# One softmax block for the second query block of the sliding attention, in a two-layer hybrid trunk on one core

## The chip, the cores and the metric

The kernel runs on one core of a Trainium2 chip. The core's engines each work through an instruction stream of their own, in order, and meet through semaphores: TensorE (PE, matrix products and transposes), VectorE (DVE), ScalarE (ACT), GpSimd (POOL) and SyncE (SP, which here issues weight loads). The metric is the device time of one execution in microseconds; lower is better.

## The reference, cut to what matters

A residual stream of 256 tokens with 1024 channels passes through two layers. Each layer projects the normalised stream once (about 12,800 columns), feeds three mixers with it (a Mamba-2 scan "ssd" with 16 heads in 4 groups, a sliding-window attention "swa" with 16 query heads and 4 key heads, a forgetting attention "fox" with 16 heads), projects and merges the three, and adds an output projection. Everything is float32. The change is in the sliding attention:

```python
# blocks of 128 queries; each sees its own and the previous block of 128 keys
scores = einsum(q_block, [previous keys, own keys]) * 64 ** -0.5     # 128 x 256 per head
diff = qi + 128 - sj
mask = (diff >= 0) & (diff < 128) & (key position >= 0)
scores = where(mask, scores, -inf)
probs  = softmax(concat([scores, sink]))[..., :-1]                    # the sink is one logit per head
out    = einsum(probs, [previous values, own values]) * silu(z)
```

The window is 128 wide. Query i of the second block therefore sees the keys j > i of the first block and the keys j <= i of its own: two triangles that together hold exactly one key for each column j. The first query block sees only the lower triangle of its own keys.

## The kernel before, in words

**Weights and dense products.** SP loads raw weights (`load_part`, up to 6 parts ahead), ACT rounds them to a high part (`hi`, L291), DVE subtracts to get a low part (`lo`, L292), and PE forms three products for each dense one (hi*hi, lo*hi, hi*lo) into PSUM tiles of the tag `mm`. Four parts are kept split ahead of use. These dense products are most of PE's work.

**PSUM.** There are eight banks of 128 x 512 float32. Three rotate under the tag `mm` (`pmm`, L75 to 76), five under `mx` (`pmx`, L78 to 79). `mx` serves all that is not a dense product: scores, transposes, value products, the scan, small sums. Each call of `pmx` takes the next of five tiles; the framework makes its first writer wait for the readers of the tile's former content.

**The attention quads.** `attn_quad` (L587 to 684) handles four heads and is called by `swa_quad` (four a layer) and `fox_quad` (four a layer). Its steps:
1. Four banks of `mx` take the scores of four heads, for query block 0 against 128 keys and for block 1 against 256 keys.
2. For each head and block, one fused DVE operation (L615) multiplies by -1/8, adds a mask or bias, takes the minimum with the sink's negative logit (swa only) and writes the result to an SBUF tile `pp`, the row minimum into `nm`. ACT then takes the exponential from `pp` to `pp` with row sums (L621).
3. For swa the sink's exponential joins the sums (L625 to L628); a reciprocal (L630) and a multiplication with 0.5 (L633) normalise `pp`.
4. After a pause `D_SOFT` (7.0), PE transposes `pp`: twelve 128 x 128 blocks in three banks (six, a pause `D_SOFT2`, six more). ACT copies each bank to SBUF (L652).
5. After `D_EVAC`, the value products of two quads are formed together, one in a bank of `mx`, one of `mm`, and DVE multiplies them onto the gate (L676).

**Others that use `mx` around it.** `ssd_group` (L804 to 862, four a layer): transposes of x for t=0 and t=1 (L816), each read by a DVE multiply (L817); the products of B and C, "cb products" (L842), read by three DVE multiplies (L845); the y products (L857), read by L860. `decay_logits` (L714 to 763): three small results in three banks, copied by ACT (L751, L756 and one after it). `group_norm` (from L904): sums of squares, read by L909. `to_hT` (L297): transposes of the stream in halves, read by ACT (L291) and DVE (L292). The start (from L1350) transposes x in quarters (`turn`, read by L1376) and runs filler transposes.

**What sets the order.** PE's order is written out by a planner in the kernel: it keeps a clock of PE costs, launches the steps above as coroutines, and lets each resume when its pause (`D_...`, in us of PE work) has passed, so that dense products stand between the score products and the transposes. Tokens limit how many quads or scan groups are open; a budget (`BUDGET`) limits how much is put between dense blocks. After the start, the order on DVE, ACT and POOL comes from the framework's scheduler. SP's order of loads follows the planner's feed. The masks (`wmask`, L203 to 210) are made on POOL at the start.

Of the kernel before, what the change touches and what calls it, by code (L numbers as in the profile page):

```python
# [28 lines left out]
T_PP, T_SSD, T_BIAS = 1, 1, 1  # L29
N_RAW, N_SPLIT = 6, 6  # L30
AHEAD = 4
WARM = 7
# [15 lines left out]
def hybrid_trunk(  # L48
# [5 lines left out]
    nc = tc.nc  # L54
# [4 lines left out]
    ps = ctx.enter_context(tc.tile_pool(name="ps", bufs=1, space=bass.MemoryType.PSUM))  # L59
# [15 lines left out]
    def pmm():  # L75
        return PS("mm", 3)

    def pmx():  # L78
        return PS("mx", 5)

    act = nc.scalar.activation
    stt = nc.vector.scalar_tensor_tensor
    tt = nc.vector.tensor_tensor
# [16 lines left out]
    def mm(o, a, b, **kw):  # L100
        n = b.free_size()
        if a.dtype == F32R:
            clock["t"] += max(0.094, n / 2350.0)
        else:
            clock["t"] += max(0.2, n / 587.0) * (0.5 if a.free_size() == 64 or a.shape[0] == 32 else 1.0)
        nc.tensor.matmul(o, a, b, **kw)  # L106

    def transpose(o, a, i):
        clock["t"] += 0.109
        nc.tensor.transpose(o, a, i)  # L110
# [74 lines left out]
    for j in range(2):  # L185
        nc.sync.dma_start(x0[:, 0, j * 512:(j + 1) * 512], x2[0:P, j * 512:(j + 1) * 512])
    ident = T("ident", [P, P])
    make_identity(nc, ident)
    tri = T("tri", [P, P])
    nc.gpsimd.memset(tri, 1.0)  # L190
    nc.gpsimd.affine_select(out=tri, in_=tri, compare_op=ALU.is_ge, fill=0.0, base=0,
                            pattern=[[1, P]], channel_multiplier=-1)
# [3 lines left out]
                            pattern=[[1, P]], channel_multiplier=-1)  # L196
# [3 lines left out]
    nc.gpsimd.tensor_copy(onesr, one)  # L200
    ones = onesr.bitcast(F32)

    wmask = T("wmask", [P, 2 * P])  # L203
    nc.gpsimd.memset(wmask, 0.0)
    nc.gpsimd.affine_select(out=wmask[:, P:2 * P], in_=wmask[:, P:2 * P],
                            compare_op=ALU.is_ge, fill=NEG, base=0,
                            pattern=[[-1, P]], channel_multiplier=1)
    nc.gpsimd.affine_select(out=wmask[:, 0:P], in_=wmask[:, 0:P],
                            compare_op=ALU.is_ge, fill=NEG, base=-1,
                            pattern=[[1, P]], channel_multiplier=-1)  # L210
    mhalf = T("mhalf", [P, 8])
    nc.gpsimd.memset(mhalf, -0.5)
    cs = T("cs", [P, 2, S])
# [125 lines left out]
    first, late = [], []  # L339
# [86 lines left out]
    for l in range(L):  # L426
        y = Layer()
# [156 lines left out]
            launch(1, swa_quad(y, g, q), D_Q)  # L584
        return rotated(y, done)

    def attn_quad(y, last, products, biases, nsink, v, vcols, sz, gated, scored=lambda: None):  # L587
# [15 lines left out]

        def score(p, i, b):
            return scs[2 * p + i][:, b * P:P + 2 * P * b]

        products(score)
        for p in range(2):
            pp = pps[p]
            ps_ = slice(4 * p, 4 * p + 4)  # L610
            ns = None if nsink is None else nsink(p)
            for i in range(2):
                for b, sl in blocks:
                    e = 4 * p + 2 * i + b
                    nc.vector.tensor_tensor_reduce(  # L615
                        out=pp[:, i, sl], in0=score(p, i, b), in1=biases(p, i, b), scale=-0.125,
                        scalar=1.0e30 if ns is None else ns[:, i:i + 1],
                        op0=ALU.add, op1=ALU.min, accum_out=nm[:, e:e + 1])
                for b, sl in blocks:
                    e = 4 * p + 2 * i + b  # L620
                    act(pp[:, i, sl], pp[:, i, sl], AF.Exp, scale=-1.0, bias=nm[:, e:e + 1],  # L621
                        accum_out=sums[:, e:e + 1])
            if nsink is not None:
                es = T("es", [P, 4], bufs=2)
                tt(es.rearrange("p (i b) -> p i b", i=2), nm[:, ps_].rearrange("p (i b) -> p i b", i=2),  # L625
                   bc(ns, 2, 2), op=ALU.subtract)
                act(es, es, AF.Exp)
                tt(sums[:, ps_], sums[:, ps_], es, op=ALU.add)  # L628
# [9 lines left out]
        order = [(0, 0), (0, 1), (1, 0), (1, 1), (0, 2), (1, 2),  # L638
                 (2, 0), (2, 1), (2, 2), (3, 0), (3, 1), (3, 2)]
        at = {hb: (n // 4, n % 4 * P) for n, hb in enumerate(order)}  # L640
        pTs = []
        for n, (h, b) in enumerate(order):
            if n == 6:
                yield D_SOFT2
            if n % 4 == 0:
                pt = pmx()
            transpose(pt[:, n % 4 * P:(n % 4 + 1) * P], pps[h // 2][:, h % 2, b * P:(b + 1) * P], ident)
            if n % 4 == 3:
                if n == 3:
                    two = T("L4", [P, 2, 512])  # L650
                pT = T("L2", [P, 512]) if n == 11 else two[:, n // 4, :]
                act(pT, pt, AF.Copy)  # L652
                pTs.append(pT)
        yield D_EVAC
        tokens["pp"] += 1

        def products_with_values(bank):
            py = bank()
            for p in range(2):
                for b, o in ((0, 0), (1, P)):  # L660
                    for i in range(2):
                        n, c = at[2 * p + i, 2 * b]
                        mm(py[64 * i:64 * i + 64, S * p + o:S * p + S], v[:, b, vcols(p, i)],
                           pTs[n][:, c:c + S - o], start=(b == 0), stop=(b == 1))
            return py


        pair.append((gated, products_with_values, sz))
        if len(pair) == 2:
            quads = pair[:]  # L670
            pair.clear()

            def values():
                for py, (_, _, own) in zip([f(bank) for (_, f, _), bank in zip(quads, (pmx, pmm))], quads):
                    o = own()
                    tt(o, py.rearrange("p (u s) -> p u s", u=2), o, op=ALU.mult)  # L676
            if not last:
                y.values.append(None)
            gates = lambda: all(g() for g, _, _ in quads)
            yield Half(gates) if last else gates  # L680
            if last:
                values()
            else:
                y.values[0] = values

    def swa_quad(y, g, q):
        yield lambda: 1 in y.sz

# [8 lines left out]
        yield from attn_quad(  # L697
            y, g == 3, products, lambda p, i, b: wmask[:, P:2 * P] if b == 0 else wmask,
            lambda p: y.nsink[:, 4 * g + 2 * p:4 * g + 2 * p + 2], y.bv,
            lambda p, i: slice(64 * g, 64 * g + 64),  # L700
            lambda: y.sz[1][:, 2 * g:2 * g + 2, :], lambda: (1, 2 * g + 1) in y.zdone)


    def logits(y, t, i, p):
# [494 lines left out]
    for y in layers:  # L1199
# [51 lines left out]
        if l == 0:  # L1251
            v, cv0, cv1 = cols(C_BV), cols(C_CV), cols(C_CV + 256)
# [8 lines left out]
        else:  # L1261
            cv0, v = cols(C_CV, 512), cols(C_BV)
# [87 lines left out]
    with tc.manual_schedule(engines={ENG.PE, ENG.DVE, ENG.Activation, ENG.Pool}):  # L1350
# [11 lines left out]
        p = pmx()  # L1362
# [98 lines left out]
        v = T("sm", [P, 8])  # L1461
# [52 lines left out]
```

## Time and profile before

| what | value |
| --- | --- |
| median of 3 runs | 820.89 us (820.74 to 822.0) |
| the profiled execution's own time | 820.72 us |
| its span in the profile | 819.0 us |
| PE busy | 808.4 us, 99% of the span |
| DVE busy | 671.5 us, 82% |
| ACT busy | 547.6 us, 67% |
| POOL busy | 172.6 us, 21% |
| transposes of `pp` (`mx<-ident,pp`) | 192, 26.3 us of PE |

How rows are read: the page's first part gives busy time, share of the span and number of instructions of each engine. A row of a group gives line, engine, operation, written tile <- read tiles, shapes, count | busy us, mean ns of one | idle time of the engine ahead of it and what ended it. A row of the waits gives who waited for whom: us in all, times, longest. A row of the chain gives start, length, engine, tile and line. A row of windows gives the window, its length, then busy time of PE, PE's weight loads, DVE, ACT and POOL, the granted TensorE clock, the share of the DMA engines and GB/s. A row of the timeline gives start, length, engine, line, operation, tiles and count. `pp<-mx,wmask,nsink` is a swa softmax, `pp<-mx,bias` a fox softmax. Matmuls are pipelined, so the time of one is longer than its share.

### The profile page before, as it was taken

The numbers are of one execution on the slowest core, as the hardware profiler recorded it, in microseconds if no ns is written. First come the engines' busy times: TensorE is split into PE (matmuls) and PEld (weight loads), VectorE is DVE, ScalarE is ACT, GpSimd is POOL, SyncE is SP. The second block draws the span as 40 slices with busy tenths as digits, with TensorE's granted clock in tenths as the row PEclk, the third lists the DMA queues.
The fourth block names the chain that finished last, engine by engine and source line by source line (L and its number), as shares of the span: only waits on it lengthen the run. The fifth ranks groups of instructions, "written<-read, shape, count | busy, mean of one in ns | idle before, by whom it ended". The sixth has DMA issues, their size and how long they took to land.

```text
span 819.0 us, 15070 instructions
## 1 busy us (share of the span) xinstructions
PE 808.4 (99%) x5242; PEld 721.2 (88%) x5242; DVE 671.5 (82%) x1468; ACT 547.6 (67%) x1186; POOL 172.6 (21%) x232
## 2 busy tenths in 40 slices
PE   8999999999999999999999999999999999999996
PEld 8998988888888988888999898889888889888896
DVE  6879899888998787965786989988899878787665
ACT  7777878775776767543666777886567767684452
POOL 3066113130210001030005621314004210102100
PEclk9999999999999999999999999999999999999999
DMA  9897869797865554866689787869868565467632
GB/s 312 278 261 193 211 187 256 190 233 214 232 206 157 180 168 148 276 208 205 221 265 265 186 222 206 228 179 259 243 206 231 155 181 163 137 208 265 206 104 77
DMA packets 141653, 170.35 MB, mean 208 GB/s; under 512 B 9314, under 2 KB 110298, under 8 KB 141578
## 3 DMA queue, kind: packets, MB, share of 16 engines
q1 hardware_dynamic: 114960, 140.53, 54.8%
q0 software_dynamic: 12928, 12.63, 9.5%
q10 hardware_dynamic: 13690, 16.24, 6.5%
q8 instruction: 41, 0.67, 0.3%
q14 instruction: 34, 0.28, 0.1%
HBM read 154.63 MB, written 2.16 MB: 191 GB/s over the span
## 4 chain that ended last, share of the span: by engine, by line
PE 85%; DVE 4%; DMA 4%; ACT 4%; issue 2%; POOL 0%; SPq 0%; ACTq 0%; DVEq 0%; POOLq 0%
PE mm L106 75%; PE mx L106 7%; PE mx L110 3%; DMA L<-cumd 2%; DVE lo L292 1%; ACT hi L291 1%; DVE L L781 1%; ACT pp L621 1%; DMA L<-L 1%; DMA raw<-in_w_in_dram 1%; DMA bias<-cumd 1%; ACT L L778 0%; ACT L L490 0%; DVE L L830 0%; POOL bias L991 0%
## 5 line engine op out<-in xcount | busy, mean ns | idle before, releaser
L292 DVE TENSOR_TENSOR lo<-raw,hi 128x1024 fp32r<-128x1024 f32 (+2 forms) x276 | 310.5, 1144 | 53.2 <-ACT hi L291 50.5
L106 PE MATMUL mm<-L,hi 128*128 128x512 f32 x1056 | 353.2, 386 | 0.0
L106 PE MATMUL mm<-hi,L 128*128 128x512 f32 (+2 forms) x1232 | 323.3, 351 | 0.1
L291 ACT ACTIVATE hi<-raw 128x1024 fp32r<-128x1024 f32 (+2 forms) x276 | 263.9, 981 | 57.2 <-PE mm L106 45.2
L106 PE MATMUL mm<-L,lo 128*128 128x256 f32 x1056 | 266.6, 273 | 0.0
L106 PEld LDWEIGHTS mm<-hi,L 128*128 128x128 f32 x1232 | 216.9, 190 | 24.1 <-issue 1.3
L106 PEld LDWEIGHTS mm<-L,hi 128*128 128x128 f32 x1056 | 194.5, 190 | 26.4 <-issue 3.2
L106 PE MATMUL mm<-lo,L 128*128 128x512 f32 (+2 forms) x616 | 213.8, 349 | 1.8 <-DVE lo L292 1.8
L106 PEld LDWEIGHTS mm<-L,lo 128*128 128x128 f32 x1056 | 202.1, 191 | 5.5
L106 PEld LDWEIGHTS mm<-lo,L 128*128 128x128 f32 x616 | 116.3, 190 | 14.1 <-DVE lo L292 2.6
L492 POOL DMA_DIRECT2D L<-L x68 | 59.4, 925 | 184.5 <-ACT L L491 151.3
L621 ACT ACTIVATE pp<-pp,nm 128x128 f32<-128x128 f32 (+1 forms) x128 | 56.5, 442 | 30.8 <-DVE nm L615 30.7
L991 POOL TENSOR_SCALAR_AFFINE_SELECT bias<-bias 128x128 f32<-128x128 f32 x64 | 34.6, 592 | 93.5 <-DMA bias<-cumd 92.7
L781 DVE SCALAR_TENSOR_TENSOR L<-L,vec,L 128x255 f32<-128x255 f32 (+2 forms) x96 | 46.2, 481 | 2.2 <-ACT L L778 0.5
L490 ACT ACTIVATE L<-mm 128x256 f32<-128x256 f32 x84 | 31.6, 376 | 15.9 <-PE mm L106 14.2
L1025 ACT ACTIVATE L<-L 128x512 f32<-128x512 f32 x24 | 15.1, 629 | 31.6 <-DVE L L1022 27.2
L633 DVE TENSOR_SCALAR pp<-pp,rsum 128x128 f32<-128x128 f32 (+1 forms) x128 | 32.5, 319 | 0.5
L492 POOL DMA_DIRECT2D qt<-L x16 | 14.5, 990 | 81.9 <-ACT qt L491 40.4
L877 DVE SCALAR_TENSOR_TENSOR L<-L,L 128x256 f32<-128x256 f32 x48 | 21.4, 449 | 8.6 <-ACT L L876 8.3
L652 ACT ACTIVATE L<-mx 128x512 f32<-128x512 f32 x48 | 26.8, 595 | 1.5 <-PE mx L110 1.5
L1070 POOL TENSOR_TENSOR L<-L,L 128x512 f32<-128x512 f32 x8 | 12.8, 1598 | 68.4 <-DVE L L1069 68.4
L912 POOL TENSOR_TENSOR sm<-sm,mhalf 128x4 f32<-128x4 f32 x8 | 8.1, 1019 | 90.5 <-DVE sm L909 90.5
(197 smaller groups left out, 841.8 us busy)
## 6 DMA issues: line engine op xcount, KB each, us to landing
raw<-in_w_in_dram SPq DMA_DIRECT2D x191, 512.0 KB, 4.7
raw<-in_w_proj_dram SPq DMA_DIRECT2D x48, 512.0 KB, 5.3
L<-L POOLq DMA_DIRECT2D x72, 128.0 KB, 5.0
raw<-in_w_out_dram SPq DMA_DIRECT2D x16, 512.0 KB, 5.1
bias<-cumd ACTq DMA_DIRECT2D x16, 256.0 KB, 3.4
L<-cumd ACTq DMA_DIRECT2D x8, 512.0 KB, 5.9
L<-in_gate_bias_dram ACTq DMA_DIRECT2D x12, 256.0 KB, 5.9
qt<-L POOLq DMA_DIRECT2D x16, 128.0 KB, 5.6
```

The source lines that it names most:

```text
L106: nc.tensor.matmul(o, a, b, **kw)
L110: nc.tensor.transpose(o, a, i)
L291: keep(act)(hi, src, AF.Copy)
L292: keep(tt)(lo, src, hi.bitcast(F32), op=ALU.subtract)
L490: act(halves(lo), ordered(p[:, S:2 * S]), AF.Copy)
L492: nc.gpsimd.dma_start(out, lo, accum_op=ALU.add)
L621: act(pp[:, i, sl], pp[:, i, sl], AF.Exp, scale=-1.0, bias=nm[:, e:e + 1], accum_out=sums[:, e:e + 1])
L633: ts(pp[:, i, sl], pp[:, i, sl], rs[:, 2 * i + b:2 * i + b + 1], 0.5, op0=ALU.mult, op1=ALU.mult)
L652: act(pT, pt, AF.Copy)
L781: stt(a[:, s:S], x_[:, 0:S - s], y.vec[:, 16 * j + u:16 * j + u + 1], a[:, s:S], op0=ALU.mult, op1=ALU.add)
L877: stt(o, th, 1.0, o, op0=ALU.add, op1=ALU.mult)
L991: nc.gpsimd.affine_select(out=bias[:, i, dst], in_=bias[:, i, src], compare_op=ALU.is_ge, fill=NEG, base=0, pattern=[[-1, P]], channel_mul ...
```

## The change

- The two triangles of a head's second-block scores are put into one 128 x 128 block. The masks are now 0/1: `later` is 1 where the key is later than the query, `other` is its transpose, for use on transposed probabilities. A predicated copy on DVE puts, for four heads at once, the first block's scores over the own block's where the key is later than the query; for the first query block it puts `least`, -1e30, there.
- The row maximum comes from a reduction over the PSUM block; the exponentials read PSUM directly, with scale 1/8; the sink's step and the normalisation are done for four heads at once. The normalisation no longer has the factor 0.5; it is in the value multiplication.
- A window quad has 8 transposes for 12. The second block's transposed probabilities are taken apart by two DVE multiplications with `other` and `tri`, one of which goes to the former block's values and one to the own block's.
- The scores are to lie in four neighbouring banks. So the five banks of `mx` become one tile, `banks`, from which `pmx` hands out the slice that was used longest ago and `pmx4` four neighbours. Fox quads take their score banks this way too; their softmax, transposes and copies are otherwise as before.
- The pause ahead of a window quad's transposes is `D_FOLD` = 8.0, and the second pause comes after four transposes. Fox quads keep `D_SOFT`.

```diff
+    banks = ps.tile([P, 5, 512], F32, tag="mx", name="mx", bufs=1)
+    oldest = list(range(5))
     def pmx():
-        return PS("mx", 5)
+        oldest.append(oldest.pop(0))
+        return banks[:, oldest[-1], :]
+    def pmx4():
+        a = 0 if oldest.index(4) > oldest.index(0) else 1
+        for i in range(a, a + 4):
+            oldest.append(oldest.pop(oldest.index(i)))
+        return banks[:, a:a + 4, :]
...
-    wmask = T("wmask", [P, 2 * P])
-    nc.gpsimd.memset(wmask, 0.0)
...
+    later, other = T("later", [P, P]), T("other", [P, P])
+    for m, way in ((later, 1), (other, -1)):
+        nc.gpsimd.memset(m, 1.0)
+        nc.gpsimd.affine_select(out=m, in_=m, compare_op=ALU.is_ge, fill=0.0, base=-1,
+                                pattern=[[way, P]], channel_multiplier=-way)
+    least = T("least", [P, 1])
+    nc.gpsimd.memset(least, NEG)
...
-        scs = [pmx() for _ in range(4)]
+        sc = pmx4()
...
+        for b in range(2) if window else ():
+            own = sc[:, :, 2 * b * P:2 * b * P + P]
+            hs = slice(4 * b, 4 * b + 4)
+            nc.vector.copy_predicated(own, bc(later, 1, 4).bitcast(mybir.dt.uint32),
+                                      sc[:, :, P:2 * P] if b else bc(least.to_broadcast([P, P]), 1, 4))
+            nc.vector.tensor_reduce(nm[:, hs], own, axis=mybir.AxisListType.X, op=ALU.max)
+            stt(nm[:, hs], nm[:, hs], -0.125, nsink, op0=ALU.mult, op1=ALU.min)
+            for h in range(4):
+                e = 4 * b + h
+                act(pps[b][:, h // 2, h % 2 * P:h % 2 * P + P], own[:, h, :], AF.Exp, scale=0.125,
+                    bias=nm[:, e:e + 1], accum_out=sums[:, e:e + 1])
+            es = T("es", [P, 4], bufs=2)
+            tt(es, nm[:, hs], nsink, op=ALU.subtract)
+            act(es, es, AF.Exp)
+            tt(sums[:, hs], sums[:, hs], es, op=ALU.add)
+            rs = T("rsum", [P, 4], bufs=4)
+            nc.vector.reciprocal(rs, sums[:, hs])
+            tt(of_heads(b), of_heads(b), bc(rs.rearrange("p (i j) -> p i j", i=2), 3, P), op=ALU.mult)
...
-        yield D_SOFT
+        yield D_FOLD if window else D_SOFT
...
+        if window:
+            first, both = T("L4", [P, 2, 512]), T("L2", [P, 512])
+            for b in range(2):
+                if b == 1:
+                    yield D_SOFT2
+                pt = pmx()
+                for h in range(4):
+                    transpose(pt[:, h * P:(h + 1) * P], pps[b][:, h // 2, h % 2 * P:h % 2 * P + P], ident)
+                ptv = pt.rearrange("p (h q) -> p h q", h=4)
+                if b == 0:
+                    act(first[:, 0, :], pt, AF.Copy)
+                else:
+                    tt(first[:, 1, :].rearrange("p (h q) -> p h q", h=4), ptv, bc(other, 1, 4), op=ALU.mult)
+                    tt(both.rearrange("p (h q) -> p h q", h=4), ptv, bc(tri, 1, 4), op=ALU.mult)
...
-                    tt(o, py.rearrange("p (u s) -> p u s", u=2), o, op=ALU.mult)
+                    po = py.rearrange("p (u s) -> p u s", u=2)
+                    if window:
+                        stt(o, po, 0.5, o, op0=ALU.mult, op1=ALU.mult)
+                    else:
+                        tt(o, po, o, op=ALU.mult)
```

More of the change, by code (lines that the diff above doesn't have):

```diff
@@ L29 @@
 T_PP, T_SSD, T_BIAS = 1, 1, 1
+D_FOLD = 8.0
 N_RAW, N_SPLIT = 6, 6
@@ L201, in hybrid_trunk @@
     ones = onesr.bitcast(F32)
-    wmask = T("wmask", [P, 2 * P])
-    nc.gpsimd.memset(wmask, 0.0)
[L205 to L210, printed above, removed]
+    later, other = T("later", [P, P]), T("other", [P, P])
[5 more added lines that the diff above has]
+    nc.gpsimd.memset(least, NEG)
     mhalf = T("mhalf", [P, 8])
@@ L585, in u_bq, with attn_quad @@
         return rotated(y, done)
-    def attn_quad(y, last, products, biases, nsink, v, vcols, sz, gated, scored=lambda: None):
+    def attn_quad(y, last, products, biases, nsink, v, vcols, sz, gated, scored=lambda: None, window=False):
         yield Half("pp")
@@ L600, in attn_quad, with of_heads @@
         blocks = ((0, slice(0, P)), (1, slice(P, 3 * P)))
-        scs = [pmx() for _ in range(4)]
+        sc = pmx4()
         def score(p, i, b):
-            return scs[2 * p + i][:, b * P:P + 2 * P * b]
+            return sc[:, 2 * p + i, b * P:P + 2 * P * b]
         products(score)
-        for p in range(2):
+        def of_heads(b):
+            return pps[b].rearrange("p i (j q) -> p i j q", j=3)[:, :, 0:2, :]
+        for b in range(2) if window else ():
[7 more added lines that the diff above has]
+                e = 4 * b + h
+                act(pps[b][:, h // 2, h % 2 * P:h % 2 * P + P], own[:, h, :], AF.Exp, scale=0.125, bias=nm[:, e:e + 1],
+                    accum_out=sums[:, e:e + 1])
+            es = T("es", [P, 4], bufs=2)
[5 more added lines that the diff above has]
+            tt(of_heads(b), of_heads(b), bc(rs.rearrange("p (i j) -> p i j", i=2), 3, P), op=ALU.mult)
+        for p in () if window else range(2):
             pp = pps[p]
             ps_ = slice(4 * p, 4 * p + 4)
-            ns = None if nsink is None else nsink(p)
             for i in range(2):
@@ L616, in attn_quad @@
                         out=pp[:, i, sl], in0=score(p, i, b), in1=biases(p, i, b), scale=-0.125,
-                        scalar=1.0e30 if ns is None else ns[:, i:i + 1],
+                        scalar=1.0e30,
                         op0=ALU.add, op1=ALU.min, accum_out=nm[:, e:e + 1])
@@ L622, in attn_quad @@
                         accum_out=sums[:, e:e + 1])
[L623 to L628, printed above, removed]
             rs = T("rsum", [P, 4], bufs=4)
@@ L634, in attn_quad @@
                        op0=ALU.mult, op1=ALU.mult)
-        yield D_SOFT
+        yield D_FOLD if window else D_SOFT
         scored()
[L638 to L645, printed above, removed]
-                pt = pmx()
[L647 to L653, printed above, removed]
+        if window:
[3 more added lines that the diff above has]
+                    yield D_SOFT2
+                pt = pmx()
+                for h in range(4):
[7 more added lines that the diff above has]
+        else:
+            order = [(0, 0), (0, 1), (1, 0), (1, 1), (0, 2), (1, 2),
+                     (2, 0), (2, 1), (2, 2), (3, 0), (3, 1), (3, 2)]
+            at = {hb: (n // 4, n % 4 * P) for n, hb in enumerate(order)}
+            pTs = []
+            for n, (h, b) in enumerate(order):
+                if n == 6:
+                    yield D_SOFT2
+                if n % 4 == 0:
+                    pt = pmx()
+                transpose(pt[:, n % 4 * P:(n % 4 + 1) * P], pps[h // 2][:, h % 2, b * P:(b + 1) * P], ident)
+                if n % 4 == 3:
+                    if n == 3:
+                        two = T("L4", [P, 2, 512])
+                    pT = T("L2", [P, 512]) if n == 11 else two[:, n // 4, :]
+                    act(pT, pt, AF.Copy)
+                    pTs.append(pT)
@@ L661, in products_with_values @@
                     for i in range(2):
-                        n, c = at[2 * p + i, 2 * b]
-                        mm(py[64 * i:64 * i + 64, S * p + o:S * p + S], v[:, b, vcols(p, i)],
-                           pTs[n][:, c:c + S - o], start=(b == 0), stop=(b == 1))
+                        h = 2 * p + i
+                        if window:
+                            m = both[:, h * P:(h + 1) * P] if b else first[:, :, h * P:(h + 1) * P]
+                        else:
+                            n, c = at[h, 2 * b]
+                            m = pTs[n][:, c:c + S - o]
+                        mm(py[64 * i:64 * i + 64, S * p + o:S * p + S], v[:, b, vcols(p, i)], m,
+                           start=(b == 0), stop=(b == 1))
             return py
@@ L675, in values @@
                     o = own()
-                    tt(o, py.rearrange("p (u s) -> p u s", u=2), o, op=ALU.mult)
+                    po = py.rearrange("p (u s) -> p u s", u=2)
+                    if window:
+                        stt(o, po, 0.5, o, op0=ALU.mult, op1=ALU.mult)
+                    else:
+                        tt(o, po, o, op=ALU.mult)
             if not last:
@@ L697, in swa_quad @@
         yield from attn_quad(
-            y, g == 3, products, lambda p, i, b: wmask[:, P:2 * P] if b == 0 else wmask,
-            lambda p: y.nsink[:, 4 * g + 2 * p:4 * g + 2 * p + 2], y.bv,
+            y, g == 3, products, None, y.nsink[:, 4 * g:4 * g + 4], y.bv,
             lambda p, i: slice(64 * g, 64 * g + 64),
-            lambda: y.sz[1][:, 2 * g:2 * g + 2, :], lambda: (1, 2 * g + 1) in y.zdone)
+            lambda: y.sz[1][:, 2 * g:2 * g + 2, :], lambda: (1, 2 * g + 1) in y.zdone, window=True)
     def logits(y, t, i, p):
```

## The prediction

> **What bounds the kernel now.** I read the head of the page first, then the chain that ended last, PE's own waits, and windows over stages with attention in them.
>
> ```profile
> span 819.0 us, 15070 instructions
> PE 808.4 (99%) x5242; PEld 721.2 (88%) x5242; DVE 671.5 (82%) x1468; ACT 547.6 (67%) x1186; POOL 172.6 (21%) x232
> PE 85%; DVE 4%; DMA 4%; ACT 4%; issue 2%; POOL 0%; SPq 0%; ACTq 0%; DVEq 0%; POOLq 0%
> PE mm L106 <- DVE lo L292: 1.8, 2, 1.2
> PE mx L110 <- POOL ident masks.py:199: 1.5, 1, 1.5
> PE mx L106 <- ACT hi L1389: 0.5, 2, 0.3
> 66.39 1.52 PE mx L106 x32
> 67.92 8.06 PE mm L106 x48
> 75.97 0.66 PE mx L110 x6
> 195.00:300.00 105.00, 105.00 (x739) 93.79 (x739) 93.87 (x247) 74.09 (x172) 13.06 (x29) 1.00 0.64 192
> 800.00:819.00 19.00, 12.63 (x82) 11.55 (x80) 10.37 (x29) 3.25 (x9) 0.00 (x0) 0.97 0.19 69
> ```
>
> PE is busy for 808.4 of 819.0 us, and the three waits listed for it come to 3.8 us. In the 105 us with fox quads and scan groups it never pauses, while DVE works 94 of them. The chain shows how that is had: score products into mx (32 in 1.52 us), then 8.06 us of dense products into mm, and only then the transposes; the dense products cover the softmax. So two things alone count: work that PE loses or gains, and waits put in front of PE's instructions. PE takes them in order, so a wait ahead of an mx write stops the dense products behind it too. The profiled execution took 820.7 us, 1.7 more than its span and 0.2 below the median of the runs, 820.89; the sum goes by 820.7.
>
> **The part that is not in the words of the change.** The pool tag mx was five rotating tiles of one bank. It becomes one tile, `banks`, of which `pmx` hands out slices. In the instruction stream of the built changed kernel the waits go by tile: a PE write into any bank of mx waits for the last DVE or ACT instruction ahead of it that reads any bank of mx. Before, it waited for the reader five banks back. Two places make it plain. The transposes of x for t=1 in a scan group (L816) follow those for t=0 without a wait before; now they wait for the multiply (L817) that reads the t=0 bank. Transposes 5 to 8 of a fox quad now wait for the copy (L652) of transposes 1 to 4, which they don't touch. I count 52 mx writes with under 2.7 us of PE work since the mx write that they wait out.
>
> **What the fold itself saves.** A window quad has 8 transposes for 12.
>
> ```profile
> L110 PE MATMUL mx<-ident,pp 128*128 128x128 f32 x192 | 26.3, 273 | 0.0
> L615 DVE CUSTOM_DVE_ANT_0 pp<-mx,wmask,nsink 128x256 f32<-128x256 f32 x32 | 15.2, 476 | 0.0
> L615 DVE CUSTOM_DVE_ANT_0 pp<-mx,wmask,nsink 128x128 f32<-128x128 f32 x32 | 11.0, 343 | 0.0
> L621 ACT ACTIVATE pp<-pp,nm 128x128 f32<-128x128 f32 x64 | 24.9, 390 | 30.5 <-DVE nm L615 30.5
> L676 DVE TENSOR_TENSOR L<-mx,L 128x512 f32<-128x512 f32 x8 | 5.5, 686 | 1.2 <-PE mx L106 1.2
> L628 DVE TENSOR_TENSOR sums<-sums,es 128x4 f32<-128x4 f32 x16 | 2.6, 160 | 0.9 <-ACT es L627 0.2
> L292 DVE TENSOR_TENSOR lo<-raw,hi 128x1024 fp32r<-128x1024 f32 x224 | 274.5, 1238 | 37.6 <-ACT hi L291 34.9 <-DMA raw<-in_w_out_dram 0.9
> ```
>
> 32 of the 192 transposes go: 32 x 26.3/192 = 4.4 us of PE, all of it on the path. The scores' and values' products stay as many. On DVE 64 fused bias-and-minimum passes (15.2 + 11.0 us) go; 16 predicated copies, 16 maxima and 16 mask multiplies of 128x512 come. The copy and the maximum are not in this trace: each lies between 0.16 (a 4-column operation) and 1.24 us (1024 columns); I take the 0.69 of L676, which also reads 512 columns of a bank. 48 x 0.69 = 33 against 26 us and 64 narrower normalisations joined to 16: about even. ACT loses half of its wide exponentials' width and 16 of 48 bank copies. None of this is on the path while PE is at 99%; were that cover gone, it is paid inside the waits below, where I count it. The masks at the start are one more memset on POOL (21% busy), behind `ident`, for which PE waits. The 8 value multiplies of window quads (L676) take the 0.5 along and keep shape and price. SP's queue of weight loads keeps its order; `D_FOLD` 8.0 for 7.0 only moves where the planner puts transposes. Each of these: nothing.
>
> **What the waits cost, bare.** That is, as if each reader started the moment PE had written. A hand-over between engines I put at 0.1 us, an estimate (an accumulator read ends at 215.94 and the exponential that needs it starts at 215.97).
>
> ```profile
> 215.86 0.08 DVE L615 DVE_READ_ACCUMULATOR2_ANT nm<- 128x1 f32 x1
> 215.97 0.51 ACT L621 ACTIVATE pp<-pp,nm 128x256 f32<-128x256 f32 x1 [0.24 <-DVE nm L615]
> L615 DVE CUSTOM_DVE_ANT_0 pp<-mx,bias 128x256 f32<-128x256 f32 x32 | 13.3, 417 | 0.0
> L615 DVE CUSTOM_DVE_ANT_0 pp<-mx,bias 128x128 f32<-128x128 f32 x32 | 9.1, 285 | 0.5 <-PE mx L106 0.5
> L615 DVE DVE_READ_ACCUMULATOR2_ANT nm<- 128x1 f32 x128 | 10.4, 82 | 0.0
> L652 ACT ACTIVATE L<-mx 128x512 f32<-128x512 f32 x48 | 26.8, 595 | 1.5 <-PE mx L110 1.5
> L817 DVE TENSOR_TENSOR L<-mx,dt 128x256 f32<-128x256 f32 x16 | 6.3, 415 | 0.0
> L845 DVE TENSOR_TENSOR L<-L,mx 128x512 f32<-128x512 f32 x24 | 15.3, 681 | 0.0
> L909 DVE TENSOR_SCALAR sm<-mx 128x4 f32<-128x4 f32 x8 | 1.1, 155 | 0.0
> L291 ACT ACTIVATE L<-mx 128x512 fp32r<-128x512 f32 x4 | 2.2, 588 | 0.0
> L292 DVE TENSOR_TENSOR L<-mx,L 128x512 fp32r<-128x512 f32 x4 | 2.7, 685 | 1.6 <-ACT L L291 1.6
> ```
>
> - Fox scores ahead of another mx write: 8 passes and 8 accumulator reads, 4 x 0.285 + 4 x 0.417 + 8 x 0.082 = 3.5, with hand-overs 3.7. Three times a scan group's y products follow at once, twice two cb products follow after 2.6 us of dense work: 3 x 3.7 + 2 x 1.1 = 13.3.
> - `decay_logits` (twice) after the third window quad's scores: its matmuls wait for that quad's last exponential. The fold works in one bank group, so the two query blocks run one after the other: copy 0.69, maximum 0.69, a 4-column step 0.16, four exponentials 1.6, twice over, with a reciprocal and a normalisation (0.2 + 0.7) and the hand-overs between (0.9): 8.1, with 2.6 covered, 5.5. Then its three small banks are written one by one, each after the copy of the one before (some 0.4 and 0.6): 6.5 a time, 13.0.
> - Fox transposes, 17 hand-overs from one bank to the next, 0.595 + 0.2 each: 13.5. x transposes, t=0 to t=1, 9 of them at 0.415 + 0.2: 5.5.
> - cb products ahead of a quad's transposes, twice three L845 and hand-overs, 2.2: 4.5. Value products ahead of scores, 4 x 0.2: 1.0. Group norm's four-column reads, and a broadcast behind one: 2.0. Two transposes of h by halves: 0.588 + 0.685 + 0.2 = 1.5 each, 3.0. The start, where the transposes of x's quarters and the filler transposes wait for one another: 2.0. Waits behind 2.6 us of other work that are nearly covered: 2.0.
>
> Sum: 13.3 + 13.0 + 13.5 + 5.5 + 4.5 + 1.0 + 2.0 + 3.0 + 2.0 + 2.0 = 59.8 us.
>
> **What the queues add.** The readers are not idle when PE has written; these rows are one fox quad of before.
>
> ```profile
> 211.99 1.58 PE L106 MATMUL mx<-qt 64*128 64x128 f32 x16
> 213.50 1.53 PE L106 MATMUL mx<-L,L 128*64 128x128 f32 x24
> 218.35 0.08 DVE L615 DVE_READ_ACCUMULATOR2_ANT nm<- 128x1 f32 x1
> 217.68 0.60 PE L110 MATMUL mx<-ident,L 128*128 128x128 f32 x4
> 220.35 0.39 DVE L817 TENSOR_TENSOR L<-mx,dt 128x256 f32<-128x256 f32 x1
> ```
>
> The y products start at 213.50, at once behind the scores; with the new wait they would have stood until 218.43, 4.9 us and not 3.7. The x transposes end at 218.28, their first reader starts at 220.35: 2.1 us late. Full lags of 2.1 at 52 places would be 109 us. But a lag is DVE's and ACT's arrears to a PE that never pauses, and each stall works them off. What is left is the instruction in hand when PE's result comes; the commonest is L292's of 1.24 us, of which half remains on the mean: 0.62 x 52 = 32 us. Window quads at the third scores have 8.2 us of cover for a chain of 8.1: 2 us each beyond it with three such arrears, 4 us.
>
> Sum: -4.4 + 59.8 + 32 + 4 = +91.4, so 820.7 + 91 = **912 us**. The Trainium skill, "Perfetto Trace Analysis", section "Optimizing Tensor Performance", Matmuls, would have independent groups rotate through PSUM banks so that the eviction of one overlaps the next group; the rotation is still written in `pmx`, and by that rule alone the sum would be -4.4. The row at 213.50 agrees with the rule for before, where the waits went by bank.
>
> **Rivals.**
> 1. *The waits cost nothing* (ends on the other side): they come early enough, or the readers finish ahead of PE wherever I counted. Then only the transposes count: 820.7 - 4.4 = 816 us. It decides if stalls stay below 4.4 us in all; against it stands that row 213.50 follows its scores with no gap. This is also what the Trainium skill's rule above would give. 0.05.
> 2. *Bare prices only*: PE's stalls clear the queues altogether. 820.7 - 4.4 + 59.8 = 876 us. For it: DVE is idle 18% of the span now, more when PE stalls. 0.20.
> 3. *A whole instruction of arrears at each place*: 1.24 x 52 = 64, and 8 at window quads: 949 us. For it: the lag of 2.1 us above, and DVE's 89% in that window. 0.22.
> 4. *The clock falls in the stalls.* In the window 800:819 the mean granted clock is 0.97 with 6.4 us of idle PE at its end: if it fell to half, it did so for 0.03 x 19/0.5 = 1.1 us, after 5.2 us of idleness. Two stalls pass that (5.5 at the logits): if half speed then lasts as long, 2 x 2.6 = 5 us more; if the three fox stalls of 3.7 pass it as well with their arrears (the 4.9 us above is near it), 5 x 2.6 = 13: 925 us. The Trainium skill, "TensorE: Matmul & The Clock Gate", Part 1, puts the window of idleness at about 3.4 us; by it the three fox stalls count even at their bare price. No row here shows a stall of that length in mid-kernel. 0.13, inside the range.
>
> **How the numbers follow.** The forecast (half an instruction of arrears, 890 to 925) has 0.40. The range runs from 864, below the bare sum by the least price of copies and maxima and some counted waits that turn out covered, to 955, above rival 3. A difference under 0.2% (1.6 us) can't be told from none. Faster 0.05, within 0.2% 0.02, slower 0.93.
>
> **What would show it.** Right: PE's busy share near 90%; among its waits mx on L615's reads, L652, L817 and the fold's exponentials, some 50 to 60 with 60 to 100 us in all, longest at `decay_logits` (5 us or more); 160 transposes from pp; DVE and ACT lags after transposes under 1 us. Wrong: PE at 99% with a span near 815 (waits by bank or harmless), a granted clock below 0.97 in attention windows (rival 4), or the copy and maximum at well over 1 us each.

## The result

The changed kernel takes 931.95 us (median of 4 runs, 930.6 to 935.84) against 821.19 us before (4 runs, 820.74 to 822.0): a ratio of 1.1355, with a 95% interval of 1.1319 to 1.1391. The forecast was 912 in a range of 864 to 955. The profiled execution of the changed kernel is the slowest of its runs: 935.84 us, of which 934.1 are its span.

The page's first lines, its row of granted clocks, and its chain by engine, after the change; behind them the row of clocks of before:

```profile
span 934.1 us, 14887 instructions
PE 846.2 (91%) x5210; PEld 742.6 (79%) x5210; DVE 681.2 (73%) x1356; ACT 543.3 (58%) x1170; POOL 161.7 (17%) x234
PEclk9999979999898997899999999899999999899999
PE 73%; DVE 11%; ACT 9%; issue 4%; DMA 3%; POOL 0%; ACTq 0%; DVEq 0%; POOLq 0%
```

```profile
PEclk9999999999999999999999999999999999999999
```

Two things are to be seen. PE idles for 87.9 us of the span where it idled for 10.6 before: 77 us. And PE is busy for 37.8 us longer with 32 instructions fewer, while the row of clocks, all nines before, has eights and sevens in it. 77 and 38 are the 115 us between the two spans.

PE's waits after the change (us in all, times, longest; lines are those of the changed kernel):

```profile
PE mx L122 <- ACT L L695: 14.4, 16, 2.1
PE mx L118 <- DVE nm L649: 11.0, 3, 5.1
PE mx L122 <- DVE L L868: 10.5, 9, 3.7
PE mx L118 <- ACT pp L634: 9.3, 2, 4.6
PE mx L118 <- DVE L L991: 5.5, 2, 2.9
PE mx L118 <- issue: 5.3, 2, 2.7
PE mx L122 <- DVE L L896: 5.1, 2, 2.6
PE mx L122 <- DVE sm L960: 4.6, 2, 2.3
```

Three waits were listed before, 3.8 us together. Now they stand where PE writes mx soon after another bank of mx was written: behind the copies of fox transposes (L695, L652 before), the fox softmax's passes (L649, L615 before), the multiplies of x (L868, L817 before), the window quad's exponentials (L634). PE stands still for longer than 0.3 us at 52 places, 79.1 us in all; before, at two places, 1.8 us (in both without the 1.5 us for the identity, `ident`, at the start and the idle time after PE's last instruction).

The fox quad that the prediction showed at 211.99 reads so in the timeline of after:

```profile
233.37 1.58 PE L118 MATMUL mx<-qt 64*128 64x128 f32 x16
237.73 0.28 DVE L649 CUSTOM_DVE_ANT_0 pp<-mx,bias 128x128 f32<-128x128 f32 x1
239.95 0.08 DVE L649 DVE_READ_ACCUMULATOR2_ANT nm<- 128x1 f32 x1
240.09 2.83 PE L118 MATMUL mx<-L,L 128*64 128x128 f32 x24 [5.13 <-DVE nm L649]
253.07 0.60 PE L122 MATMUL mx<-ident,pp 128*128 128x128 f32 x4
253.76 0.60 ACT L695 ACTIVATE L<-mx 128x512 f32<-128x512 f32 x1
254.41 0.44 PE L122 MATMUL mx<-ident,pp 128*128 128x128 f32 x2 [0.75 <-ACT L L695]
```

The y products (the row with 24 matmuls) followed the scores at once before. Now they start 0.06 us after the quad's last accumulator read has ended, 5.13 us later. They also take 2.83 us where the same 24 took 1.53: that is the second loss, the clock. At 254.41 the transposes of the second bank wait for the copy of the first, 0.75 us.

The clock behind one of the two waits at the decay logits, by windows (length; busy us of PE, PE's loads, DVE, ACT, POOL; granted clock; DMA share; GB/s):

```profile
122.25:125.66 3.41, 2.87 (x32) 2.15 (x32) 2.27 (x4) 0.00 (x0) 0.00 (x0) 0.50 0.76 256
129.08:132.49 3.41, 0.00 (x0) 0.00 (x0) 3.39 (x10) 2.29 (x10) 0.86 (x1) 0.99 0.28 43
132.49:139.32 6.83, 5.39 (x20) 3.84 (x21) 1.53 (x5) 1.67 (x8) 0.00 (x0) 0.50 0.02 5
139.32:142.73 3.41, 3.41 (x22) 3.12 (x22) 1.73 (x3) 2.57 (x6) 0.56 (x1) 1.00 0.03 11
```

PE does nothing from 129.08 to 132.49 and runs at half speed for the 6.83 us after that. The trace has 13 such stretches inside the kernel, each 3.41 or 6.83 us long, 71.7 us together; half of that is 35.8 us. PE is busy in 64.3 of the 71.7; if its work there takes twice its time, the clock costs some 32 us, an estimate. That is not all of the 37.8 us, from which the transposes that went have already been taken off (3.5 us, as fold_banks shows below). Some 9 us more of PE's busy time come with the stalls themselves: where PE runs on, a matmul overlaps the one before it and adds 0.156 us to PE's busy time on the mean; the 45 at full speed that start behind a gap of over 0.03 us add 0.35 us each.

### The profile page after: what moved, and what is told of

The parts are those of the page before. It is cut to its first block, busy times and chain, and to the rows that moved or that the text cites. A ratio compares the mean times of both kernels' runs of the same rounds, so it can differ in the third digit from the quotient of the medians.

```text
span 934.1 us, 14887 instructions
## 1 busy us (share of the span) xinstructions
PE 846.2 (91%) x5210; PEld 742.6 (79%) x5210; DVE 681.2 (73%) x1356; ACT 543.3 (58%) x1170; POOL 161.7 (17%) x234
## 4 chain that ended last, share of the span: by engine, by line
PE 73%; DVE 11%; ACT 9%; issue 4%; DMA 3%; POOL 0%; ACTq 0%; DVEq 0%; POOLq 0%
PE mm L118 63%; PE mx L118 6%; PE mx L122 4%; DVE lo L303 3%; ACT hi L302 2%; DMA L<-cumd 2%; DVE L L832 1%; ACT pp L634 1%; ACT L L695 1%; DVE pp L649 1%; DMA L<-in_x_dram 1%; ACT pp L655 1%; DVE mx L628 1%; DVE nm L630 1%; DVE L L896 1%
## 5 line engine op out<-in xcount | busy, mean ns | idle before, releaser
L118 PE MATMUL mm<-L,hi 128*128 128x512 f32 x1056 | 365.5, 396 | 0.0
L118 PEld LDWEIGHTS mm<-L,hi 128*128 128x128 f32 x1056 | 200.6, 195 | 29.3 <-issue 5.3
L118 PEld LDWEIGHTS mm<-L,lo 128*128 128x128 f32 x1056 | 208.4, 197 | 6.1
L122 PE MATMUL mx<-ident,pp 128*128 128x128 f32 x160 | 28.2, 293 | 26.6 <-ACT L L695 14.4
L1042 POOL TENSOR_SCALAR_AFFINE_SELECT bias<-bias 128x128 f32<-128x128 f32 x64 | 25.0, 475 | 122.6 <-DMA bias<-cumd 89.7
L122 PEld LDWEIGHTS mx<-ident,pp 128*128 128x128 f32 x160 | 19.3, 146 | 32.9 <-ACT L L695 18.4
L634 ACT ACTIVATE pp<-mx,nm 128x128 f32<-128x128 f32 x64 | 22.6, 364 | 31.4 <-DVE nm L631 31.4
L655 ACT ACTIVATE pp<-pp,nm 128x128 f32<-128x128 f32 x64 | 28.2, 441 | 15.2 <-DVE nm L649 15.2
L122 PE MATMUL mx<-ident,L 128*128 128x128 f32 (+2 forms) x101 | 18.7, 294 | 16.8 <-DVE L L868 9.9
L118 PE MATMUL mx<-L,L 128*64 128x128 f32 (+1 forms) x256 | 21.2, 321 | 11.0 <-DVE nm L649 11.0
L963 POOL TENSOR_TENSOR sm<-sm,mhalf 128x4 f32<-128x4 f32 x8 | 10.6, 1332 | 115.6 <-DVE sm L960 115.6
```

The lines of the kernel that those rows point to most:

```text
L634: act(pps[b][:, h // 2, h % 2 * P:h % 2 * P + P], own[:, h, :], AF.Exp, scale=0.125, bias=nm[:, e:e + 1], accum_out=sums[:, e:e + 1])
L963: nc.gpsimd.tensor_tensor(r0[:, 0:4], v[:, 0:4], mhalf[:, 0:4], op=ALU.pow)
L1042: nc.gpsimd.affine_select(out=bias[:, i, dst], in_=bias[:, i, src], compare_op=ALU.is_ge, fill=NEG, base=0, pattern=[[-1, P]], channel_mul ...
```

## Experiments

The theory after the result: (A) waits by tile cost some 77 us of stalls, and (B) the clock, which falls in them, another 32 to 36; the fold itself saves a little. Rivals: the fold's serial softmax is what costs (against A), and the lower clock costs nothing since the waits set the time (against B).

### The one tile without the fold: one_tile

```diff
 (kernel before)
+    banks = ps.tile([P, 5, 512], F32, tag="mx", name="mx", bufs=1)
+    turns = [0]
     def pmx():
-        return PS("mx", 5)
+        turns[0] += 1
+        return banks[:, turns[0] % 5, :]
```

> The kernel before with one edit: the five rotating banks of mx become slices of one tile; the softmax of the sliding attention, its 12 transposes and its masks stay. Theory (waits by tile, and the clock that falls in them): the same stalls as in the changed kernel, less at the decay logits (the scores are released by DVE's eight fused passes, not by exponentials, some 5 us less in all), more at the copies of window quads, which now have three banks of transposes (16 more at about 0.75 us, 12 us): 77 us of waits and about 30 us of lost clock, 925 us (905 to 945). Rival (the fold's serial softmax is what costs): within 10 us of before, 820 to 830. A middle value would divide the loss between the two.

Measured: 948.9 us, ratio 1.1573 (1.1552 to 1.1593). These few lines of tiling, with no part of the fold, cost more than the whole change. PE's largest waits:

```profile
PE mx L114 <- ACT L L656: 42.6, 32, 3.4
PE mx L114 <- DVE L L821: 14.7, 9, 4.3
PE mx L110 <- DVE nm L619: 9.9, 5, 4.4
```

The rival (820 to 830) is out. The size was 24 us off: the 16 additional hand-overs between window quads' transposes cost not 12 but 27 us (of the 42.6 us at L656, 27.3 lie in window quads), since those copies start late: one starts 2.8 us after its transposes have ended. Against this kernel the fold *saves* 17 us; a window quad of the changed kernel has two banks of transposes with the second pause between them, and none of its copies is among the waits.

### The fold without the one tile: fold_banks

```diff
 (changed kernel)
+    def pmx():
+        return PS("mx", 5)
+    def pmx4():
+        return [pmx() for _ in range(4)]
...
+            own = [s[:, 2 * b * P:2 * b * P + P] for s in sc]
             hs = slice(4 * b, 4 * b + 4)
-            nc.vector.copy_predicated(own, ...four heads...)
-            nc.vector.tensor_reduce(nm[:, hs], own, ...)
+            for h in range(4):
+                nc.vector.copy_predicated(own[h], later.bitcast(mybir.dt.uint32),
+                                          sc[h][:, P:2 * P] if b else least.to_broadcast([P, P]))
+                nc.vector.tensor_reduce(nm[:, 4 * b + h:4 * b + h + 1], own[h], axis=mybir.AxisListType.X, op=ALU.max)
```

> The changed kernel with five one-bank tiles again: the four heads' scores lie in four tiles, and the predicated copy and the maximum are done head by head (128x128, 64 of each for 16). Theory (waits by tile are the whole loss): 32 transposes less than before, 820.9 - 4.4 = 816.5, plus up to 4 us each at the two decay logits, whose third bank is now held until an exponential has read it: 816 to 826, PE at 98 to 99%, granted clock 0.99 or more. Rival (the fold's chain outlasts its cover of 8 to 10 us of dense work in every window quad): stalls of 2 us or more ahead of the eight quads' transposes, 835 us or more.

Measured: 836.3 us, ratio 1.0187 (1.0166 to 1.0208). 96 of the 111 us are gone, stalls and lost clock together, so A holds for most of the loss. But the expectation, 816 to 826 with a clock of 0.99 or more, was missed: the fold ends above before, and 836.3 with a clock of 0.988 lies in the rival's range. Its PE line and waits, and the transposes:

```profile
PE 812.2 (97%) x5210; PEld 722.0 (86%) x5210; DVE 681.9 (81%) x1452; ACT 535.8 (64%) x1170; POOL 167.6 (20%) x234
PE mx L110 <- ACT acum L795: 12.9, 2, 6.4
PE mx L114 <- DVE pp L635: 2.7, 2, 2.0
L114 PE MATMUL mx<-ident,pp 128*128 128x128 f32 x160 | 22.8, 273 | 2.7 <-DVE pp L635 2.7
```

The expected stall at the decay logits is there, 6.4 us where up to 4 were allowed for, and costs half-speed stretches as well (17 us of them, at most 8.5 lost, counting one behind the 2.0 us wait). By the profile the second product waits for the copy of the first (L795), which stands in ACT's order behind the exponentials; and those wait for the maxima of four heads. The rival's stalls ahead of window quads' transposes come to 2.7 us, so they are real and small: the time is the rival's, the place is not. What the rival had right is that the fold's softmax costs by itself: fold_banks is some 15 us slower than before with no joined tile.

### Useless work in the stalls: fill

```diff
 (changed kernel)
+    def fill(n):
+        p = pmm()
+        for _ in range(n):
+            nc.tensor.transpose(p[:, 0:P], ident, ident)
...
             y.values.pop()()
+            if window:
+                fill(20)
...
         yield D_CUM
+        fill(30)
         pa = pmx()
...  (in fox_quad's products)
+            if y.l == 0 and j < 6:
+                fill(20)
```

> The changed kernel with useless transposes of the identity put ahead of the waits in three places: 30 (about 3.2 us) ahead of each decay_logits, 20 (2.1 us) after the value products of window quads, 20 after the scores of three fox quads of layer 0. They are written to a bank of mm that nobody reads. Theory (the clock falls after an idle stretch of 2 us or more and stays at half for 3.4 or 6.8 us): the waits end as early as before, the clock stays at full speed in those places, 10 to 15 us less than the changed kernel, 917 to 923. Rival (PE's slower clock comes from elsewhere or costs nothing, as the waits set the time): 930 to 937, as the fillers lie inside the waits or add to them.

Measured: 921.3 us (921.05 to 922.03), as expected, 10.6 less than the changed kernel, with 160 more instructions on PE. The stretch of the first decay logits, changed kernel first and this one second:

```profile
118.00:144.00 26.00, 17.96 (x127) 14.13 (x123) 15.71 (x38) 10.41 (x35) 2.58 (x3) 0.80 0.38 101
```

```profile
118.00:144.00 26.00, 23.55 (x192) 20.73 (x189) 17.59 (x41) 13.57 (x41) 4.62 (x9) 1.00 0.56 148
```

With work in the stall the clock stays at 1.00. Over the trace the loss to half speed falls from 38.3 to 23.4 us (both with the end of the kernel, where PE is done). B holds: adding work made the kernel faster, so the clock is a cost beside the waits.

### One wait taken away: logits_mm

```diff
 (changed kernel, decay_logits)
-        pa = pmx()
+        pa = pmm()
...
-        pr = pmx()
+        pr = pmm()
...
-        pf = pmx()
+        pf = pmm()
```

> The changed kernel with the three small products of decay_logits in banks of mm in place of mx, which takes away their waits for the quad's exponentials and for one another. Theory: the stalls of 4.6 us at each of the two and 0.9 us between the banks go (11 us), and with them the clock's fall behind them (half speed for 10.2 and 6.8 us, 8.5 us lost): 912 to 918 us, and only part of it if the wait is met again by the next write to mx behind 5 us of dense work. Rival (the wait only moves to that next write): 925 to 932.

Measured: 921.9 us median, but 915.67 to 923.54. In the profiled execution, the shortest of its runs (span 913.9), PE's stalls over 0.3 us fall from 79.1 to 68.4 us, the 11 us that were expected, and the loss to the clock by 9. That the stalls are gone, and not met again, is shown; the median lies between the two expectations. The spread of 0.9%, where before has 0.3% in the same round, is the clock's: the granted clock was 0.969 in the run of 915.67 us, 0.965 in that of 920.92 and 0.961 in those of 922.9 and 923.54. One less the clock, times the span, is 28.3, 32.2, 35.9 and 35.9 us, and the span less that is 885 to 887 us in all four; in the changed kernel it is 894 to 897. So the edit takes away 9 us in every run, and how much half speed is left differs from run to run, in two of them as much as in the changed kernel (34 to 37 us). That this goes by the place of a stall in a 3.41 us window is likely, but no run here tells it apart.

### Making the fold pay

The next five kernels ask whether the fold can be had without its price. fold_logits puts the second and third product of decay_logits into one bank of mm, with both copies behind both products; fold_logits_d10 adds a longer pause; before_logits has that edit of decay_logits alone, without the fold.

```diff
 (fold_banks -> fold_logits, decay_logits)
-        pr = pmx()
+        pr = pmm()
...
-        act(cum[:, 0, :], pr[0:16, 0:S], AF.Copy)
-        pf = pmx()
+        pf = pr[:, S:2 * S]
...
+        act(cum[:, 0, :], pr[0:16, 0:S], AF.Copy)
         act(cum[:, 1, :], pf[0:16, 0:S], AF.Copy, scale=-8.0)
 (fold_logits -> fold_logits_d10)
-D_FOLD = 8.0
+D_FOLD = 10.0
```

> fold_banks (five one-bank tiles, the fold head by head) with the second and third product of decay_logits in one bank of mm, and both their copies after both products. It takes away the two waits of 6.45 us that fold_banks shows there (12.9 us) and the half-speed stretches behind them (13.7 us long, 6.8 us lost): 836.3 - 19.7 = 816.6, 814 to 820, faster than before by the 32 transposes (4.4 us). Rival (the wait moves on: dense products meet the bank of mm before it is read): 825 to 836.

> The same with D_FOLD 10.0 for 8.0, for the waits of 2.0 and 0.8 us ahead of window quads' first transposes that fold_banks shows, with a half-speed stretch of 3.4 us behind one. Theory: up to 4.5 us less than fold_logits, 812 to 817. Rival (a longer pause delays what follows in the plan, and dense work runs out elsewhere): 818 or more.

> The kernel before with the same edit of decay_logits alone. No wait stands at that place in the trace of before, so no change: 819.5 to 821.5. If it were faster by several us, a gain of fold_logits would not be the fold's.

Measured: fold_logits 826.5 us, 1.0066 (1.0043 to 1.0089); fold_logits_d10 832.72, 1.0132 (1.0112 to 1.0153); before_logits 822.66, 1.0007 (0.9993 to 1.0021), no difference. fold_logits and fold_logits_d10 missed their expectations and lie in their rivals' ranges. The two waits of 6.4 us went, and a smaller one took their place, as the rival said. The largest waits of fold_logits:

```profile
PE mm L110 <- ACT L L494: 3.1, 2, 1.6
PE mx L114 <- DVE pp L635: 1.9, 1, 1.9
PE mx L110 <- DVE da L788: 1.2, 2, 0.6
```

L494 is the eviction of an ordinary dense product. ACT takes it in order, behind exponentials that wait for the fold's maxima; so a dense product now waits for the fold, 1.6 us twice. (Some 3 us of the miss are no wait: the 19.7 us to be gained were read in the slowest run of fold_banks, 839.39, and taken off its median.) The longer pause did not help: fold_logits_d10 has 6.7 us of waits for L494, six times.

Hence the last pair. fold_heads does the softmax head by head: one predicated copy in the second block, then the fused pass of before on both blocks, which writes to SBUF, and exponentials from there (`lowm` masks the first block, `flat` is all zeros). fold_heads_logits adds the edit of decay_logits.

```diff
 (fold_banks -> fold_heads, softmax of a window quad, for each head i of pair p)
+                own = score(p, i, 1)[:, P:2 * P]
+                nc.vector.copy_predicated(own, later.bitcast(mybir.dt.uint32), score(p, i, 1)[:, 0:P])
+                for b, s_, m in ((0, score(p, i, 0), lowm), (1, own, flat)):
+                    e = 4 * p + 2 * i + b
+                    nc.vector.tensor_tensor_reduce(
+                        out=pp[:, i, b * P:b * P + P], in0=s_, in1=m, scale=-0.125, scalar=ns[:, i:i + 1],
+                        op0=ALU.add, op1=ALU.min, accum_out=nm[:, e:e + 1])
+                for b in range(2):
+                    e = 4 * p + 2 * i + b
+                    act(pp[:, i, b * P:b * P + P], pp[:, i, b * P:b * P + P], AF.Exp, scale=-1.0,
+                        bias=nm[:, e:e + 1], accum_out=sums[:, e:e + 1])
```

> fold_banks with its softmax head by head throughout: per head one predicated copy for the second block, then the fused scale-mask-minimum pass of before on both blocks (with a mask for the first, zeros for the second), which writes to SBUF, and the exponentials from SBUF; one normalisation for two heads. The scores' banks come free after DVE's passes as in before, and an exponential waits for its own head alone. Theory (what fold_banks lost were the banks held for exponentials and the chain over four heads): the waits of 6.45 us at the decay logits, and the evictions late behind exponentials, go: 815 to 820, up to 3.5 us (32 transposes) less than before. Rival (DVE, with some 1 us more for each window quad, is now what dense work waits for): 822 to 828.

> fold_heads with the edit of decay_logits from fold_logits. Theory: nothing is left to save there, within 1.5 us of fold_heads. If it is faster by 3 us or more, the small banks still waited for score banks.

Measured: fold_heads 823.62 us, 1.0024 (1.0011 to 1.0037); fold_heads_logits 819.49 us, 0.9978 (0.9966 to 0.9989), which is faster than both kernels, by 0.2% against before. PE in fold_heads, its largest wait, then the same of fold_heads_logits:

```profile
PE 808.8 (98%) x5210; PEld 720.6 (88%) x5210; DVE 675.2 (82%) x1468; ACT 540.7 (66%) x1170; POOL 168.6 (21%) x236
PE mx L110 <- DVE nm L624: 4.1, 4, 1.8
```

```profile
PE 805.7 (98%) x5210; PEld 718.9 (88%) x5210; DVE 675.1 (82%) x1468; ACT 537.7 (66%) x1170; POOL 171.1 (21%) x236
PE mm L110 <- ACT L L497: 2.9, 2, 1.5
```

fold_heads missed its 815 to 820, and not for the rival's reason: no dense product (mm) is among its waits. The decay logits still wait for DVE's passes over the score banks, 1.8 us twice, and each wait is followed by a half-speed stretch of 3.41 us. Whether these passes are late for the copies that DVE has in addition is not told apart. The edit of decay_logits was expected to save nothing more, within 1.5 us; it takes both waits and both stretches away, and the median falls by 4.1 us. As before_logits changed nothing, the 2 us below before are the fold's: 32 transposes less, minus some waits.

## Why the prediction was right, and where its sum was not

**The mechanism.** "A PE write into any bank of mx waits for the last DVE or ACT instruction ahead of it that reads any bank of mx": shown, by one_tile and fold_banks from both sides. The 52 places counted answer to 52 stalls over 0.3 us, though not place for place, so that the equal count is partly chance. Rival 1 (waits that cost nothing, 816) is out.

**The saving.** 4.4 us by the group's busy time; fold_banks shows the 160 transposes at 22.8 us against 26.3, 3.5 us.

**The waits, bare and arrears.** Forecast 59.8 + 32 + 4 = 96 us, measured 77. The terms, from the rows above:
- Fox copies, 13.5: 14.4. The first fox hand-over, 0.75, is the bare price (0.595 and two hand-overs); 14.4/16 = 0.9 leaves little for arrears.
- x transposes, 5.5: 10.5. Here the arrears stayed, up to 3.7 us.
- Fox scores, 13.3: 11.0. The chain of eight passes was sized at 3.5 by adding mean durations; in the timeline it runs from 237.73 to 240.03, 2.3 us, because starts overlap. Arrears of up to 2.8 us ahead of it made good for that. The two cb products that were to wait 1.1 us each do not show among PE's waits.
- Decay logits, 13.0: 9.3 at the exponentials, and 1.5 between the small banks by their rows.
- cb products, 4.5: 5.1 (L896).
- Undersized: value products ahead of scores, 1.0, took 5.3 (the row with "issue", 2 x 2.66; each ends 0.1 us behind DVE's multiply of the value products, which starts some 3 us after they have ended), group norm, 2.0, took 10.9 with its broadcasts (L960 4.6 and 0.8, L991 5.5), the transposes of h by halves, 3.0, took 4.8 (3.4 and 1.4), and the start, 2.0, took 3.2 (L1427).

Arrears of half an instruction of 1.24 us at each place were too many: 77 less the 60 bare leaves 17 us, 0.33 a place. A stall does work off DVE's and ACT's queues, as rival 2 (876) said, only not everywhere; a whole instruction of arrears at each place, rival 3, is further off than the half.

**The clock.** This is the term that the sum left out. It stood among the rivals at 5 to 13 us with the condition of 5.2 us without work, read from the one place of before where PE had ended. Measured: some 32 us (the granted clock, with the end of the kernel, takes 36.8 us more off than before), and the condition is lower (below). The Trainium skill's page "TensorE: Matmul & The Clock Gate", Part 1, speaks of an idle window of about 3.4 us; the trace has windows of that length, 3.41 us, but here a window need not be idle throughout: about 2 us of idle PE in it were enough (last section).

**The balance.** The two profiled spans differ by 115 us, the forecast by 91. Waits were put 19 us too high; the clock's 32, the 9 us of matmuls that start behind a gap, and 0.9 of the saving were missing. 912 lies as near to 932 as it does partly by luck, because errors of opposite sign met; the mechanism of the waits does not rest on that.

**The fold's softmax.** It was costed at nothing, "paid inside the waits" if the cover is gone. In the changed kernel that is so. In fold_banks its cover held at the transposes of six of the eight window quads (2.7 us of waits at the other two), and the chain over four heads was paid elsewhere: by what stands behind it on ACT.

**The copy and the maximum** were taken at 0.69 each between 0.16 and 1.24. Measured in the changed kernel:

```profile
L630 DVE TENSOR_REDUCE nm<-mx 128x4 f32<-128x512 f32 x16 | 11.0, 691 | 0.3
L628 DVE COPY_PREDICATED_SCALAR mx<-later,least 128x512 f32 x8 | 6.0, 750 | 1.4 <-PE mx L118 1.3
L628 DVE COPY_PREDICATED mx<-later,mx 128x512 f32<-128x512 uint32 x8 | 5.5, 692 | 3.3 <-ACT pp L634 3.3
```

**The parts at nothing**, masks on POOL and SP's queue, brought no new row among PE's waits (the 1.5 us for `ident` stood there before).

## What to carry to other kernels

Before several rotating buffers are joined into one tile for the sake of a wider instruction, look at what the framework's waits go by: here joining five banks cost 128 us by itself, to save 12 DVE operations in each quad. On an engine that is busy 99% of the time, count every place where it writes the joined tile, and price the clock with the stalls: here it added nearly half of their cost (some 32 us to 77). A fold that shortens the busy engine's work pays only if the engines it loads keep their order; done head by head, with the small products moved out of its way, it gave 0.2% here.

## What the runs showed of the hardware

- The granted clock goes by windows of 3.41 us, and a window need not be empty. In the traces of after, one_tile, fill, logits_mm, fold_banks, fold_heads and fold_logits each window, on the grid of the clock's records, that had run at full speed and in which PE was idle for 2.0 us or more was followed by half speed; none with less than 1.8 us was; between the two both occur. The half speed then lasts one or two windows, and so a stall of 2 us can cost 1.7 to 3.4 us more behind it.
- A predicated copy of 128x512 in PSUM takes 0.69 us with a tensor as source and 0.75 with a value repeated from one column; for 128x128 it is 0.29 and 0.35 us (fold_banks' edit, in the trace of fold_logits).
- Fused passes with their accumulator reads follow each other faster than their durations add up: eight of each in 2.3 us, where the durations sum to 3.5.
